# An expert layer whose elementwise work all runs on VectorE, with GpSimd left to gather rows, and the tables of a state space layer made in another place

## The chip, the core and the metric

The kernel runs on one core of a Trainium2 chip. A core has five engines with queues of their own, each worked off in order: TensorE (PE in the rows; PEld is its weight load), VectorE (DVE), ScalarE (ACT), GpSimd (POOL) and SyncE (SP), which here only issues DMAs. Matmuls write PSUM; everything else works in SBUF. The metric is the device time of one execution in microseconds.

## What is computed

Two blocks of a network run over 512 tokens of width 1024, in f32. The first is a mixer followed by a layer of product-key experts; the second is attention, a squared-ReLU MLP, a state space layer (S5) and another such MLP, each followed by a layer norm. What matters here is the expert layer, the first MLP and the tables that the S5 layer reads:

```python
def peer(h, wq, k1, k2, u, v):
    q = (tok @ wq).reshape(-1, 8, 2, 128)                  # 8 heads
    v1, i1 = lax.top_k(q[:, :, 0] @ k1.T, 16); v2, i2 = ...
    cand = v1[..., :, None] + v2[..., None, :]
    top_s, top_c = lax.top_k(cand, 16)
    expert = i1[top_c // 16] * 128 + i2[top_c % 16]        # of 16384 experts
    gate = softmax(top_s)
    act = gelu(sum(x * u[expert]))                         # 128 experts per token
    return sum(gate * act * v[expert])

def sq_relu_mlp(h, w1, b1, w2, b2):
    a = relu(h @ w1 + b1)
    return (a * a) @ w2 + b2

# S5: for 64 groups of 64 states, exp(a dt), cos, sin and products with b and c
# give the tables with which the scan over the tokens is done
```

## The kernel before

Every f32 product is made of three products of a "high" and a "low" part: `split` (L363) takes a weight block of 128x1024 that a DMA brought (`raw`), casts it on ScalarE to `whi` (L366) and subtracts on an elementwise engine to give `wlo` (L367). `eng` chooses that engine: VectorE, unless GpSimd is passed. `proj` and `mm3` then issue 24 matmuls for a block (8 k-chunks, three products each). Activations are split in the same way (`split_act`: cast L493 on ScalarE, subtraction L494 on VectorE, tiles `ahi` and `alo`).

The expert layer `peer` treats 384 of the 512 tokens densely and 128 by gathering.

- **Dense tokens.** The 16384 experts are 128 chunks of 128. For a chunk, `hidden` makes the 24 matmuls `pu` of `u` with the tokens, then a GELU on ScalarE into `hx`. The first `len(AHEAD)` chunks, 80 of them, are made while the experts are being chosen, and written to DRAM (`he`). The rest follow later, in line.
- **Choosing.** `select` makes the scores (`ps_q`) and the top 16 on VectorE (`rank`, `experts`). `spread` then builds a gate for every token and expert chunk with one-hot matrices (L1320, L1321 on VectorE, L1323 and L1329 on ScalarE, `pg` matmuls L1327) and writes them to DRAM (`gd`).
- **Groups.** `grouped` goes over 16 groups of 8 chunks. For each chunk `act` brings `hx` back or makes it, multiplies it by its gates (L1063), and `split_act` makes `ahi` and `alo`, in 9 buffers each. Eight blocks of `v` with 24 matmuls `ps` each follow, and `emit` adds the result to `res` (L1096).
- **Gathered tokens.** `gathered` is a generator that is advanced between the other steps: 128 times an indirect DMA on GpSimd's queue brings one row of `u` per token (L1102) and VectorE reduces it against the token (L1123), then 128 times a row of `v` is fetched and added (L1138). These VectorE instructions are kept in program order. Three `rows` buffers are shared by all.
- **Tables.** `s5_tables` is another generator, advanced between groups 6 to 14. It has about 300 small VectorE instructions, some of ScalarE and TensorE (L1719, L1742), and DMAs of its results to DRAM. `S5In` loads the first two of eight sets of tables at the start of the first MLP.

The first MLP (`mlp`) works in four groups of 8 chunks as well: 24 matmuls `ps_f` a chunk, ReLU on ScalarE, the square on GpSimd (L1416), the split, then 8 blocks with 24 matmuls `ps`. Beside it `mod_columns` computes 48 columns of a modulation by 96 VectorE reductions (L519) over tiles `modw`, which have two buffers and are kept in program order.

The order on each engine is not the order of the code: the framework's scheduler places instructions by a time line of its own, except those kept in order.

## Time and profile before

| what | value |
|---|---|
| median of 3 runs | 3735.75 us (3727.42 to 3742.15) |
| profiled execution | 3738.89 us |
| its span | 3737.1 us |
| busy in the span | PE 3429.7 (92%), DVE 2611.3 (70%), ACT 1601.4 (43%), POOL 1417.7 (38%) us |
| DMA | 635 MB, mean 170 GB/s |

The stages, from the span's start: the mixers end at about 1019 us; choosing experts and spreading gates runs to 1650; the groups to 2507; attention to 2698; the layer norm and the first MLP to 3087; the S5 layer and the second MLP to the end. A matmul counts as busy until its modelled end, so a busy PE is an upper bound of its work.

### The profile page before, as it was taken

How to read it: one execution, taken by the hardware profiler on the slowest of the kernel's cores; microseconds unless marked ns; L12 is line 12 of the kernel's file. 1: busy time of each engine (PE TensorE's matmuls, PEld its weight loads, DVE VectorE, ACT ScalarE, POOL GpSimd, SP SyncE). 2: the span in 40 equal slices, each digit the busy share in tenths (PEclk: the TensorE clock that was granted, in tenths of full speed). 3: DMA queues.
4: the chain of work that ended last, by engine and by line, in shares of the span. 5: the costliest groups of instructions: out<-in, count | busy, mean ns of one | idle time of the engine just before them, and what ended most of it. 6: DMA issues, size and time to landing. Idle time of an engine off the chain costs nothing.

```text
span 3737.1 us, 49602 instructions
## 1 busy us (share of the span) xinstructions
PE 3429.7 (92%) x18337; PEld 3000.6 (80%) x18337; DVE 2611.3 (70%) x4302; ACT 1601.4 (43%) x2482; POOL 1417.7 (38%) x1020
## 2 busy tenths in 40 slices
PE   8999989998998699968899998988989998899998
PEld 5888878877888699958889988986677777777886
DVE  5566675355559999979988989877586536774334
ACT  5565634563332259953333333343442233243333
POOL 3111100111235567745566656544071116353113
PEclk9999999999999899979999998999999999799999
DMA  5223273114325658886888888861156533722332
GB/s 198 80 91 97 88 261 107 51 46 151 100 93 183 203 171 323 309 293 229 287 288 286 286 295 278 276 208 64 34 169 199 185 107 113 203 91 90 96 95 69
DMA packets 264530, 634.97 MB, mean 170 GB/s; under 512 B 33440, under 2 KB 111392, under 8 KB 263904
## 3 DMA queue, kind: packets, MB, share of 16 engines
q1 hardware_dynamic: 216672, 489.18, 39.9%
q0 software_dynamic: 38144, 138.43, 10.5%
q10 hardware_dynamic: 9472, 4.20, 0.4%
q8 instruction: 144, 2.36, 0.3%
q14 instruction: 98, 0.80, 0.1%
HBM read 572.51 MB, written 63.39 MB: 170 GB/s over the span
## 4 chain that ended last, share of the span: by engine, by line
PE 34%; DVE 9%; DMA 6%; issue 5%; POOL 4%; ACT 4%; SPq 0%; POOLq 0%; ACTq 0%; DVEq 0%
PE ps L379 18%; PE ps_f L379 7%; PE ps L412 2%; DMA modw<-in_modT_dram 2%; POOL rows L1102 2%; DVE gacc L1138 1%; ACT o L1323 1%; DVE wlo L367 1%; PE pu L379 1%; DMA raw<-in_u_dram 1%; POOL hx L1063 1%; ACT gs L1329 1%; PE ps_g L379 1%; POOL wlo L367 1%; DVE nx L285 1%
## 5 line engine op out<-in xcount | busy, mean ns | idle before, releaser
L366 ACT CAST whi<-raw 128x1024 fp32r<-128x1024 f32 x547 | 573.1, 1050 | 1031.4 <-PE ps L379 344.8
L367 DVE TENSOR_TENSOR wlo<-raw,whi 128x1024 fp32r<-128x1024 f32 x389 | 501.0, 1291 | 269.5 <-ACT whi L366 154.9
L367 POOL TENSOR_TENSOR wlo<-raw,whi 128x1024 fp32r<-128x1024 f32 x158 | 406.6, 2578 | 231.3 <-ACT whi L366 137.2
L379 PE MATMUL ps<-ahi,whi 128*128 128x384 f32 (+2 forms) x1560 | 349.7, 362 | 98.4 <-ACT ahi L493 80.4
L379 PEld LDWEIGHTS ps<-ahi,whi 128*128 128x128 f32 x1560 | 281.6, 196 | 133.5 <-ACT ahi L493 91.6
L379 PE MATMUL ps<-alo,whi 128*128 128x384 f32 (+2 forms) x1560 | 341.0, 357 | 16.9 <-DVE alo L494 16.8
L379 PE MATMUL ps<-ahi,wlo 128*128 128x384 f32 (+2 forms) x1560 | 325.9, 351 | 0.0
L379 PEld LDWEIGHTS ps<-alo,whi 128*128 128x128 f32 x1560 | 285.5, 196 | 40.1 <-DVE alo L494 19.9
L379 PEld LDWEIGHTS ps<-ahi,wlo 128*128 128x128 f32 x1560 | 276.7, 191 | 20.9 <-issue 0.2
L1416 POOL TENSOR_TENSOR relu<-relu 128x512 f32<-128x512 f32 x64 | 87.5, 1368 | 506.6 <-ACT relu L1415 502.1
L1102 POOL DMA_INDIRECT rows<-in_u_rows_dram,gidx x128 | 181.0, 1414 | 218.2 <-DVE gact L1123 125.4
L1102 POOL DMA_INDIRECT rows<-in_v_rows_dram,gidx x128 | 175.3, 1370 | 199.9 <-DVE gacc L1138 174.4
L1123 DVE CUSTOM_DVE_ANT_0 rows<-rows,gx 128x1024 f32<-128x1024 f32 x128 | 234.9, 1843 | 9.2 <-DMA rows<-in_u_rows_dram,gidx 9.2
L379 PE MATMUL pu<-h_hi,wlo 128*128 128x384 f32 x1024 | 210.6, 347 | 26.1 <-POOL wlo L367 26.1
L379 PE MATMUL pu<-h_hi,whi 128*128 128x384 f32 x1024 | 209.9, 346 | 21.1 <-ACT hx L1041 21.1
L1138 DVE SCALAR_TENSOR_TENSOR gacc<-rows,ggate,gacc 128x1024 f32<-128x1024 f32 x127 | 207.1, 1631 | 25.0 <-DMA rows<-in_v_rows_dram,gidx 24.7
L379 PEld LDWEIGHTS pu<-h_hi,wlo 128*128 128x128 f32 x1024 | 184.4, 194 | 29.9 <-POOL wlo L367 29.9
L379 PEld LDWEIGHTS pu<-h_hi,whi 128*128 128x128 f32 x1024 | 184.2, 194 | 24.3 <-ACT hx L1041 23.3
L379 PE MATMUL pu<-h_lo,whi 128*128 128x384 f32 x1024 | 202.8, 338 | 0.0
L379 PEld LDWEIGHTS pu<-h_lo,whi 128*128 128x128 f32 x1024 | 180.4, 189 | 0.2 <-issue 0.2
L1063 POOL TENSOR_TENSOR hx<-gt,hx 128x384 f32<-128x384 f32 x128 | 158.1, 1247 | 46.5 <-ACT hx L1041 27.1
L1356 DVE SCALAR_TENSOR_TENSOR res<-ps,mod,res 128x512 f32<-128x512 f32 (+1 forms) x92 | 62.2, 677 | 143.0 <-PE ps L379 132.9
(617 smaller groups left out, 7476.1 us busy)
## 6 DMA issues: line engine op xcount, KB each, us to landing
raw<-in_u_dram SPq DMA_DIRECT2D x128, 512.0 KB
raw<-in_v_dram SPq DMA_DIRECT2D x128, 512.0 KB
raw<-in_w_dram SPq DMA_DIRECT2D x128, 512.0 KB
modw<-in_modT_dram SPq DMA_DIRECT2D x192, 256.0 KB
gd<-gs SPq DMA_DIRECT2D x32, 768.0 KB
gt<-gd SPq DMA_DIRECT2D x32, 768.0 KB
raw<-in_w_hg_dram SPq DMA_DIRECT2D x32, 512.0 KB
res<-in_adaT_dram SPq DMA_DIRECT2D x64, 256.0 KB
```

The lines of the kernel that those rows point to most:

```text
L285: nc.vector.scalar_tensor_tensor(out=t[:], in0=res[:, k, tok], scalar=self.g[:, k:k + 1], in1=r[:], op0=ALU.mult, op1=ALU.mult)
L366: self.nc.scalar.copy(out=hi[:], in_=raw[:])
L367: (eng or self.nc.vector).tensor_tensor(out=lo[:], in0=raw[:], in1=hi[:].bitcast(F32), op=ALU.subtract)
L379: self.nc.tensor.matmul(ps, lhsT=w[a], rhs=x[b], start=start and n == 0, stop=stop and n == last)
L412: self.nc.tensor.matmul(ps[:, tok], lhsT=w[a][:, k], rhs=rhs(k, b, tok), start=(k == 0 and i == 0), stop=(k == 7 and i == 2))
L1063: nc.gpsimd.tensor_tensor(out=xb, in0=gt, in1=xb, op=ALU.mult)
L1102: self.nc.gpsimd.indirect_dma_start(out=t[:], out_offset=None, in_=self.ia[rows], in_offset=bass.IndirectOffsetOnAxis(ap=self.gidx[:, s:s ...
L1123: i = nc.vector.tensor_tensor_reduce(out=r[:], in0=r[:], in1=x[:], scale=1.0, scalar=0.0, op0=ALU.mult, op1=ALU.add, accum_out=act[:, s:s ...
L1138: i = nc.vector.scalar_tensor_tensor(out=acc[:], in0=r[:], scalar=w, in1=acc[:], op0=ALU.mult, op1=ALU.add)
L1323: nc.scalar.activation(out=o2[:, j], in_=o2[:, j], func=AF.Copy, scale=gt[:, t0 + j:t0 + j + 1])
L1356: self.nc.vector.scalar_tensor_tensor(out=self.res[:, d, tok], in0=ps, scalar=self.gate1(n)[:, d:d + 1], in1=self.res[:, d, tok], op0=ALU. ...
L1416: nc.gpsimd.tensor_tensor(out=r[:], in0=r[:], in1=r[:], op=ALU.mult)
```

## The change

GpSimd keeps only the gathers in the expert layer: the `wlo` subtraction of 13 query blocks and 128 `u` blocks and the 128 gate products go to VectorE. `rows` has six buffers in place of three. 96 chunks are made ahead in place of 80. The tables are made in the first MLP, from its chunks 1, 4, 7 to 31, and `S5In` loads the first two sets before its last group's tail. A few scratch tiles share a buffer to make room.

```diff
-AHEAD = [8 * g + i for i in range(8) for g in range(16)][:80]
+AHEAD = [8 * g + i for i in range(8) for g in range(16)][:96]
+ROWS = 6
...
         self.B, self.M, self.got = B, M, {}
-        for c in range(2):
-            self.load(c)
...
-            def hidden(e, out, eng=None):
-                w = self.weights(ia["u"][e], eng=eng)
+            def hidden(e, out):
+                w = self.weights(ia["u"][e])
...
-                hidden(e, x[:], nc.gpsimd)
+                hidden(e, x[:])
                 nc.sync.dma_start(out=he[i], in_=x[:])
...
-                        hidden(e, x[:], nc.gpsimd)
+                        hidden(e, x[:])
                     xb = x[:].rearrange("p (b t) -> p b t", b=GBLK)
-                    nc.gpsimd.tensor_tensor(out=xb, in0=gt, in1=xb, op=ALU.mult)
+                    nc.vector.tensor_tensor(out=xb, in0=gt, in1=xb, op=ALU.mult)
...
-                tabs = [tc.tile_pool(name="s5t", bufs=1), tc.tile_pool(name="s5tp", bufs=1, space=PSUM)]
-                tables = self.s5_tables(*[p.__enter__() for p in tabs], self.s5dram)
...
-                    if 6 <= g < 15:
-                        next(tables, None)
...
-        t = self.A.tile([128, D], F32, tag="rows", bufs=3, name="rows")
+        t = self.A.tile([128, D], F32, tag="rows", bufs=ROWS, name="rows")
...
-                    w = self.weights(ia["w_q"][hd * 2 + p], eng=nc.gpsimd)
+                    w = self.weights(ia["w_q"][hd * 2 + p])
...
-        m = M.tile([128, n], F32, tag=f"rest{n}", bufs=3, name="rest")
+        m = M.tile([128, n], F32, tag=f"rest{n}", bufs=2, name="rest")
...
-            if n == 1:
-
-                ins = self.tc.tile_pool(name="s5in", bufs=1)
-                self.tables = S5In(self, ins.__enter__())
...
             row = self.mod_row(mt, ia["crow2"])
             modT = ia["modT"].rearrange("a b p k -> (a b) p k")
+            tabs = [self.tc.tile_pool(name="s5t", bufs=1), self.tc.tile_pool(name="s5tp", bufs=1, space=PSUM)]
+            tables = self.s5_tables(*[p.__enter__() for p in tabs], self.s5dram)
...
                 self.mod_columns(mt, row, modT, range(48 + 2 * f, min(96, 50 + 2 * f)), self.col("modb", 0, 96), self.mod2)
+                if f % 3 == 1:
+                    next(tables, None)
...
             if g == 3 and i == 0:
-                mods.__exit__(None, None, None)
+                for p in tabs[::-1] + [mods]:
+                    p.__exit__(None, None, None)
+                self.ins = self.tc.tile_pool(name="s5in", bufs=1, side="right")
+                self.tables = S5In(self, self.ins.__enter__())
+                for c in range(2):
+                    self.tables.load(c)
```

**GpSimd in the groups.** Ahead of the change, this is its queue over about one group: gathers (`rows`), gate products (`hx`) and the low parts of `u` blocks (`wlo`) in turn.

```order
L1063 TENSOR_TENSOR hx<-gt,hx 128x384 x4
L1102 DMA rows<-in_v_rows_dram,gidx 128x1024
L1063 TENSOR_TENSOR hx<-gt,hx 128x384
L1102 DMA rows<-in_v_rows_dram,gidx 128x1024 x3
L367 TENSOR_TENSOR wlo<-raw,whi 128x1024
L1102 DMA rows<-in_v_rows_dram,gidx 128x1024 x2
L367 TENSOR_TENSOR wlo<-raw,whi 128x1024 x2
```

With the change this is its queue for the whole expert layer, with the last instruction ahead of it (of the first three query blocks) and the first behind it (of the attention's first blocks). Line numbers are now those of the changed kernel.

```order
L366 TENSOR_TENSOR wlo<-raw,whi 128x1024 x3
L1093 DMA rows<-in_u_rows_dram,gidx 128x1024 x128
L1093 DMA rows<-in_v_rows_dram,gidx 128x1024 x128
L366 TENSOR_TENSOR wlo<-raw,whi 128x1024 x3
```

Nothing but gathers stands between the two.

**VectorE where one group ends and the next begins.** Before: the low halves `alo` of the next group's activations, with gathered sums (`gacc`), one `wlo` of a `v` block and pieces of the tables (`s_...`) between them.

```order
L1138 SCALAR_TENSOR_TENSOR gacc<-rows,ggate,gacc 128x1024
L494 TENSOR_TENSOR alo<-hx,ahi 128x384 x3
L1738 COPY s_bbz<-s_bb_17038 64x4x16 x2
L1744 COPY s_kz<-spk 32x4x128
L1463 SCALAR_TENSOR_TENSOR s_rot<-s_an 128x256
L1738 COPY s_bbz<-s_bb_17039 64x4x16
L494 TENSOR_TENSOR alo<-hx,ahi 128x384
L1738 COPY s_bbz<-s_bb_17039 64x4x16
L1138 SCALAR_TENSOR_TENSOR gacc<-rows,ggate,gacc 128x1024
```

With the change, at the same place:

```order
L493 TENSOR_TENSOR alo<-hx,ahi 128x384 x2
L366 TENSOR_TENSOR wlo<-raw,whi 128x1024
L1129 SCALAR_TENSOR_TENSOR gacc<-rows,ggate,gacc 128x1024
L366 TENSOR_TENSOR wlo<-raw,whi 128x1024
L1062 TENSOR_TENSOR hx<-gt,hx 128x384
L1129 SCALAR_TENSOR_TENSOR gacc<-rows,ggate,gacc 128x1024
L366 TENSOR_TENSOR wlo<-raw,whi 128x1024
L1062 TENSOR_TENSOR hx<-gt,hx 128x384
L493 TENSOR_TENSOR alo<-hx,ahi 128x384
```

The tables are gone, and the gate products and the `wlo` of the `u` blocks stand between the `alo` of one group. On TensorE the matmuls `pu` that lie at each such border are 72 before and 48 now.

**VectorE in the first MLP**, in the eight `w2` blocks of the first group. Before: the result (`res`), the low half of the next block, and the modulation's reductions (`modw`).

```order
L519 ISA modw,mod_89<-modw,sc_row_23698,cols 128x512
L519 ISA mod_89 128x1
L1356 SCALAR_TENSOR_TENSOR res<-ps,mod_89,res 128x512
L367 TENSOR_TENSOR wlo<-raw,whi 128x1024
L519 ISA modw,mod_89<-modw,sc_row_23699,mod_89 128x512
```

With the change:

```order
L1343 SCALAR_TENSOR_TENSOR res<-ps,mod_89,res 128x512
L366 TENSOR_TENSOR wlo<-raw,whi 128x1024
L1729 SCALAR_TENSOR_TENSOR s_cp<-s_cp,s_t_23362 128x576
L1700 TENSOR_TENSOR s_an<-s_tr,s_iota 128x256
L518 ISA modw,mod_89<-modw,sc_row_23028,mod_89 128x512
L518 ISA mod_89 128x1
L1343 SCALAR_TENSOR_TENSOR res<-ps,mod_89,res 128x512
L366 TENSOR_TENSOR wlo<-raw,whi 128x1024
L518 ISA modw,mod_89<-modw,sc_row_23027,cols 128x512
```

The tables' instructions stand between the reductions and ahead of the next `wlo`. The first part of the tables, about a hundred instructions of 32 to 512 elements, stands earlier still, among those of the layer norm ahead of this MLP.

## Rows read from the trace of the kernel before

**Rows 1.** Stages: start:end, length, busy us (instructions) of PE, PEld, DVE, ACT, POOL; PEclk, DMA share, GB/s

```profile
1019.00:1631.00 612.00, 544.47 (x3193) 519.24 (x3193) 543.68 (x1182) 360.29 (x701) 370.48 (x179) 0.95 0.64 218
1111.00:1320.00 209.00, 159.46 (x836) 154.12 (x835) 208.30 (x757) 58.50 (x77) 117.49 (x62) 0.90 0.60 189
1374.00:1631.00 257.00, 241.75 (x1607) 236.90 (x1605) 241.32 (x202) 246.90 (x545) 179.24 (x89) 0.98 0.84 302
1650.00:2507.00 857.00, 768.75 (x4234) 745.54 (x4233) 765.36 (x896) 303.51 (x411) 503.04 (x343) 0.95 0.80 272
2698.00:3087.00 389.00, 370.06 (x1691) 301.66 (x1690) 241.35 (x385) 128.78 (x168) 104.69 (x92) 0.98 0.52 165
```

**Rows 2.** PE in 1650:2507: busy us, mean ns | idle before, and who ended it

```profile
L379 PE MATMUL ps<-ahi,whi 128*128 128x384 f32 x962 | 215.9, 359 | 98.4 <-ACT ahi L493 80.4 <-issue 8.0 <-DVE res L1096 5.0
L379 PE MATMUL ps<-alo,whi 128*128 128x384 f32 x960 | 202.8, 350 | 8.2 <-DVE alo L494 8.2
...
L1742 PE MATMUL spk<-s_cp,s_bbz 128*32 128x128 f32 x128 | 17.0, 276 | 0.0
L1719 PE MATMUL spt<-ident,s_s 128*128 128x128 f32 x64 | 12.6, 317 | 0.0
```

**Rows 3.** Waits in 1640:2507: who waited for whom, total us, times, longest us

```profile
ACT ahi L493 <- POOL hx L1063: 206.5, 60, 17.3
```

**Rows 4.** Timeline from 1990 us: start, length in us, engine, line, operation

```profile
1995.15 0.48 ACT L1041 ACTIVATE hx<-pu 128x384 f32<-128x384 f32 x1
1995.42 1.28 DVE L1138 SCALAR_TENSOR_TENSOR gacc<-rows,ggate,gacc 128x1024 f32<-128x1024 f32 x1
1996.19 1.32 POOL L1102 DMA_INDIRECT rows<-in_v_rows_dram,gidx  x1 [0.30 <-issue]
...
2003.41 0.55 DVE L494 TENSOR_TENSOR alo<-hx,ahi 128x384 fp32r<-128x384 f32 x1
...
2004.60 3.75 DVE L1714 TENSOR_TENSOR s_s<-s_s,s_t 128x512 f32<-128x512 f32 x1
2004.84 2.96 POOL L1063 TENSOR_TENSOR hx<-gt,hx 128x384 f32<-128x384 f32 x3
...
2009.94 1.21 DVE L367 TENSOR_TENSOR wlo<-raw,whi 128x1024 fp32r<-128x1024 f32 x1
```

**Rows 5.** DVE in 1650:2507, by line: busy us, mean ns | idle before

```profile
L1138 DVE SCALAR_TENSOR_TENSOR gacc<-rows,ggate,gacc 128x1024 f32<-128x1024 f32 x127 | 207.1, 1631 | 25.0 <-DMA rows<-in_v_rows_dram,gidx 24.7
L367 DVE TENSOR_TENSOR wlo<-raw,whi 128x1024 fp32r<-128x1024 f32 x122 | 163.2, 1339 | 7.3 <-ACT whi L366 6.4 <-PE pu L379 0.9
L494 DVE TENSOR_TENSOR alo<-hx,ahi 128x384 fp32r<-128x384 f32 x128 | 106.2, 849 | 36.8 <-ACT ahi L493 35.2 <-issue 1.4
L1123 DVE CUSTOM_DVE_ANT_0 rows<-rows,gx 128x1024 f32<-128x1024 f32 x47 | 78.7, 1678 | 4.5 <-DMA rows<-in_u_rows_dram,gidx 4.5
L1096 DVE SCALAR_TENSOR_TENSOR res<-ps,mod,res 128x384 f32<-128x384 f32 x122 | 74.1, 608 | 30.5 <-PE ps L379 29.5 <-PE ps L412 0.5
```

**Rows 6.** DVE in 1080:1640, by line

```profile
L1123 DVE CUSTOM_DVE_ANT_0 rows<-rows,gx 128x1024 f32<-128x1024 f32 x81 | 156.2, 1939 | 4.8 <-DMA rows<-in_u_rows_dram,gidx 4.8
L1320 DVE TENSOR_TENSOR o<-tr,iota 128x1024 f32<-128x1024 f32 x48 | 70.5, 1471 | 11.4 <-PE pg L1327 8.0 <-issue 2.2 <-ACT gs L1329 0.9
L1321 DVE TENSOR_TENSOR o<-tr,iota 128x1024 f32<-128x1024 f32 x48 | 67.0, 1395 | 0.5 <-PE pt L1298 0.5
```

**Rows 7.** Chain that ended last: start us, length us, engine, tile and line, matmuls

```profile
2166.04 21.08 PE ps L379 x120
...
2485.90 12.70 PE pu L379 x72
```

**Rows 8.** Waits in 2690:3160, which holds the first MLP

```profile
DVE modw L519 <- DMA modw<-in_modT_dram: 61.1, 46, 3.2
```

**Rows 9.** GpSimd in 2690:3160, its costliest line

```profile
L1416 POOL TENSOR_TENSOR relu<-relu 128x512 f32<-128x512 f32 x32 | 42.4, 1326 | 261.1 <-ACT relu L1415 256.6 <-DVE alo L494 4.6
```

**Rows 10.** DMA queue SP in 1650:2507: what its issues waited for

```profile
SPq L1745 <- DVE s_kz L1744: 32.5, 7, 10.7
```

More of the change, by code (lines that the diff above doesn't have):

```diff
@@ L1081, in between @@
                             pass
-                    if 6 <= g < 15:
-                        next(tables, None)
-                    if g == 15:
-                        for p in tabs[::-1]:
-                            p.__exit__(None, None, None)
                 def emit(d, ps, tok):
@@ L1110, in gathered @@
         x = A.tile([128, D], F32, tag="gx", bufs=1, name="gx")
-        f = A.tile([128, D], F32, tag="rows", bufs=3, name="gf")
+        f = A.tile([128, D], F32, tag="rows", bufs=ROWS, name="gf")
         nc.vector.tensor_tensor(out=f[:].rearrange("p (k t) -> p k t", k=8), in0=self.h[0][:, :, GATHERED].bitcast(F32),
@@ L1237, in experts @@
             v = nc.vector
-            new = lambda name, dt=F32: S.tile([128, n], dt, tag=f"{name}{n}", bufs=1, name=name)
+            new = lambda name, dt=F32: S.tile([128, n], dt, tag=f"{name}", bufs=1, name=name)
             flat = lambda t: t[:, c0:c1].rearrange("p c h r -> p (c h r)")
@@ L1255, in experts @@
                 key = new(f"key{p}")
-                num = S.tile([128, n], F32, tag=f"num{n}", bufs=1, name="num")
+                num = S.tile([128, n], F32, tag="num", bufs=1, name="num")
                 v.tensor_copy(out=num[:], in_=flat(idx[p]))
@@ L1267, in experts @@
                 out.append(key)
-            gate, den = new("gate"), S.tile([128, n // 16], F32, tag=f"den{n}", bufs=1, name="den")
+            gate, den = new("gate"), S.tile([128, n // 16], F32, tag="den", bufs=1, name="den")
             h16 = lambda a: a[:].rearrange("p (h r) -> p h r", r=16)
@@ L1346, in block2 @@
         for n in range(4):
-            if n == 1:
-                ins = self.tc.tile_pool(name="s5in", bufs=1)
-                self.tables = S5In(self, ins.__enter__())
             if n == 3:
-                ins.__exit__(None, None, None)
+                self.ins.__exit__(None, None, None)
             with self.tc.tile_pool(name=f"lay{n}", bufs=1) as M, \
```

## The prediction

> **What bounds the kernel now.** I read the stages first, since an average over the whole span mixes different limits [rows 1]. Two of the changed stages are bound by TensorE: the groups (768.75 of 857 us busy) and the first MLP (370.06 of 389). Choosing and spreading is mixed: over all of it PE and DVE are busy alike (544.47 and 543.68 of 612 us), but from 1111 to 1320 VectorE is full (208.30 of 209), and from 1374 to 1631 ScalarE is (246.90 of 257). The granted clock is 0.95 to 0.98 over the TensorE-bound stages, so their matmuls run near the upper level, and I change nothing for it.
>
> Next I read what the idle TensorE of the groups waits for. 857 - 769 leaves 88 us, and the waits for `ahi` (80.4) and `alo` (8.2) make up all of it [rows 2]. `ahi` is ScalarE's cast, and ScalarE in turn waited 206.5 us, up to 17.3 us at a time, for GpSimd's gate product `hx` [rows 3]. So the stage has a queue behind it that the change empties: the product on GpSimd behind gathers and `wlo`.
>
> Last I read single durations, because the same VectorE instruction has two prices [rows 4]. `gacc` beside a gather on GpSimd takes 1.28 us; `s_s`, half as large, takes 3.75 us beside three products on GpSimd. Alone, `alo` takes 0.55 and `wlo` 1.21. The means in the groups are above these: `gacc` 1.631, `alo` 0.849, `wlo` 1.339 [rows 5]; while the experts are chosen, the gathered reduction takes 1.939 and the one-hot build 1.471, both of 128x1024 elements [rows 6]. VectorE pays for a GpSimd that computes, and hardly for one that gathers.
>
> **Prices.** A matmul of 384 columns costs 21.08/120 = 0.176 us on the chain, and 12.70/72 = 0.176 where the inline chunks stand [rows 7]. On VectorE I take the prices without GpSimd: 1.28 for `gacc`, 1.21 for `wlo` and for the other operations of 128x1024, 0.55 for `alo`. The gate product on VectorE is not in the trace. It has the shape and the two SBUF inputs of `alo`, hence 0.55; the mean of `alo` as it is now, 0.849, bounds it above.
>
> **Choosing and spreading.** 16 more chunks are made here, 384 matmuls: 67.6 us. PE then has 544.5 + 67.6 = 612 us of work in a stage of 612, so all of it must fit the present holes. VectorE gains 111 `wlo` (13 query blocks and the 98 chunks that now stand ahead of the first group's matmuls): 134 us. It loses the surcharge: 81 x (1.939 - 1.21) = 59 us on the reductions and 48 x (1.471 - 1.21) = 12 on L1320, with some more on its twin L1321 and on smaller operations, which I don't count. 544 + 134 - 71 = 607 of 612. Both engines are near full, and neither is over: the low bound is 0. The high bound is what the two full stretches would add if nothing of it found a hole: while VectorE is full, 836 matmuls, or 35 chunks, are made [rows 1], and their `wlo` are 35 x 1.21 = 42 us; while ScalarE is full, 16 more GELUs of 0.48 are 8 us. That makes +50. I take **+18**, about a third of it: the surcharge goes in the first of these stretches too, and ScalarE loses 20 of its 160 loads of activation tables in the change, 12 of them at the GELU's line, which help to pay for the second.
>
> **The groups.** PE loses 24 matmuls at each of 15 borders and those of one chunk of the first group: 384 x 0.176 = 67.6 us, and the tables' transposes and products, 17.0 + 12.6 = 29.6 us [rows 2]. 768.75 - 97.2 = 671.5 us of matmuls are left. Of the idle 88 us I keep 50. At each of 15 borders, the last inline chunk goes through GELU (0.48), product (0.55), cast (about 0.5, as a tile of the same size in the GELU) and `alo` (0.55), 2.1 us, and in VectorE's queue a `gacc` or a `wlo`, some 1.2 us, stands ahead of one of these: 3.3 x 15 = 50. The cover for the chunks before it shrinks too: from 72 matmuls (12.7 us) to 48 (8.4), in which VectorE has seven `alo`, up to two products, and the `gacc` and `wlo` between them, some 10 us at the prices alone. Most of the `alo` of chunks that come from DRAM can stand earlier, in the group before, as one buffer more than a group needs exists.
>
> Whether VectorE keeps up decides the rest. Its bill in the groups: `gacc` 127 x 1.28 = 163, the 47 reductions x 1.21 = 57, `wlo` (122 + 30) x 1.21 = 184, `alo` 128 x 0.55 = 70, products 128 x 0.55 = 70, `res` 122 x 0.608 = 74. Together 618 us, below 671.5. The tables are no longer in it: they are the difference between 765.36 and the five lines' 629.3, **136 us** [rows 1, 5]; I use 130, as some pairs of small results of other lines are in it. So PE bounds the groups: 671.5 + 50 = 721, a gain of 857 - 721 = **-136 us**. Bounds: with the present 88 us of idle, 760 and -97; with VectorE at today's means (127 x 1.631 + 47 x 1.678 + 152 x 1.339 + 128 x 0.849 twice + 74 = 781) at least 781 and some 9 of idle, so -67; with 19 us of idle in place of 50, -167. Loads: 272 GB/s over 857 us is 233 MB; less 16 blocks of `u` of 0.5 MB it is 225, in 721 us 312 GB/s. The spread stretch moves 302 at a share of 0.84 [rows 1], so the queues carry it, without much reserve.
>
> **The first MLP.** PE gets the tables' 29.6 us. VectorE gets their 130 us: 241 + 130 = 371 of 389, not counting that its reductions stand still for `modw` for 61.1 us [rows 8], since they have two buffers and a fixed order; 371 + 61 = 432. The tables' DMAs now stand in SyncE's queue beside those of `modw` and the weights. In the groups that queue stood 32.5 us in seven waits for `s_kz` [rows 10]; here a load behind such a wait comes late by up to 10.7 us, and the cover is the raw buffers ahead. What waits behind the tables on VectorE are the next block's `wlo`, and so PE. I take 29.6 plus as much idle again as the stage has, 389 - 370 = 19: **+49**; the sum of VectorE, 432 - 389 = 43, lies beside it. Low bound: PE's 29.6 fill the 19 first, +11. High bound: 432 and the whole of the 42.4 us in which GpSimd squares [rows 9], as a lock on VectorE, +85.
>
> On this term a rule of the Trainium skill speaks against the change. Rows 4 show a table instruction with two SBUF inputs at 3.75 us beside GpSimd's products, and `gacc` unchanged beside a gather. The skill's page "SBUF — State Buffer", section "Who interferes with whom", says that a VectorE instruction with two SBUF inputs contends with a GpSimd instruction that reads SBUF, that the second to issue blocks fully, and that one that only writes does no harm. By it the squares in the MLP, whose input and output are in SBUF, would lock the tables as the products did in the groups, and the term would be +85, the time 3706; by the rows alone it is +49. The trace of before has no table instruction beside a square, so it neither agrees nor speaks against it. I give this case 0.15 of the forecast's 0.55 below.
>
> **The sum.** 18 - 136 + 49 = -69. Against the profiled execution of 3738.9 this is **3670 us**; the median of the runs lies 3 us lower, 3667, which I count as the same.
>
> **The rivals.**
>
> First, VectorE inherits the wait. Products stand in a strict queue behind `gacc`, and `gacc` itself waits for gathers (24.7 us of VectorE's idle time now [rows 5]); ScalarE then waits for VectorE as it did for GpSimd, the 88 us stay, and in the MLP the tables hold up `wlo` at the high bound. For it: the order at the borders puts two `gacc` and three `wlo` among the last products. Against it: six `rows` buffers instead of three, and GpSimd free of all else. 18 - 97 + 85 = +6: 3745 us, the same. Chance 0.17.
>
> Second, slower: the two prices of VectorE have another cause than GpSimd's arithmetic, say the traffic of the gathers or of the weights, and stay. It decides when `gacc` stays near 1.6 us with only gathers on GpSimd. Then choosing has 544 + 134 = 678 us of VectorE in 612, +66; the groups are bound by VectorE, 790, -67; the MLP is at +85. Together +84: 3823 us. For it: the means are averages, and traffic grows. Against it: the 1.28 us beside a gather [rows 4]. Chance 0.13.
>
> Third, more than forecast: the waits at the borders shrink to 19 us and choosing costs nothing, since the surcharge was larger than what I counted, and the MLP costs only PE's matmuls, 30. -167 + 30 = -137: 3602 us. For it: at 618 of 671 VectorE has slack, and the product's queue is two instructions deep. Against it: 8.4 us of cover instead of 12.7. Chance 0.15.
>
> **How the numbers follow.** The forecast has 0.55, with its terms anywhere between their bounds. About 0.5%, 19 us, is what a measurement of this kernel can tell from no change. Faster: the forecast nearly whole, the third rival, and a little of the first, 0.73; the same, most of the first and the edge of the forecast, 0.13; slower, the second and the edge of the first, 0.14. The range reaches from the third rival, 3600, to just over the first, 3755; outside lie the second and the half of the third that goes further.
>
> **What would show it.** In the changed profile: on GpSimd only gathers between the third query block and the attention; `gacc` near 1.28, `alo` near 0.55, `wlo` near 1.21, the reductions near 1.21 (at today's means the second rival is right). The groups last about 721 us and PE waits for `ahi` and `alo` for some 50 (near 88 is the first rival, below 20 the third). Choosing to the first group lasts about 18 us longer. From the attention's end to the S5 layer it takes about 438 us, PE waiting for `wlo`, VectorE still for `modw`. The forecast falls if the MLP grows by over 85 us, if the squares lock the tables, or if the groups become bound by loads at some 300 GB/s.

## The result

The changed kernel takes 3599.89 us in the median (3597.06 to 3603.72), against 3737.02 (3727.42 to 3742.15) for the kernel before: a ratio of 0.964, interval 0.9615 to 0.9658, 137 us or 3.7% less. The forecast was 3670; the low end of the range, 3600, was missed by a tenth of a microsecond. The sign was as forecast, and TensorE still bounds the groups and the MLP as forecast; the gain is twice as large, and nearly all of the miss lies in the groups. The profiled execution takes 3601.07 us, its span 3599.3.

The stages of the changed kernel, in the columns of [rows 1], cut at the events that cut them there:

```profile
1017.00:1631.00 614.00, 593.78 (x3577) 572.71 (x3577) 516.03 (x1290) 386.16 (x733) 121.03 (x85) 0.99 0.69 239
1110.00:1313.00 203.00, 201.05 (x1158) 200.01 (x1157) 199.45 (x804) 79.15 (x104) 37.48 (x30) 1.00 0.74 247
1375.00:1631.00 256.00, 237.88 (x1587) 232.21 (x1585) 206.42 (x231) 245.12 (x538) 77.92 (x52) 0.98 0.81 300
1646.00:1700.00 54.00, 40.77 (x199) 38.68 (x200) 41.45 (x71) 12.24 (x17) 21.54 (x17) 0.80 0.82 278
1646.00:2310.00 664.00, 643.35 (x3656) 637.49 (x3657) 572.52 (x763) 230.13 (x312) 251.58 (x171) 0.98 0.89 317
1700.00:2290.00 590.00, 582.58 (x3341) 578.84 (x3340) 517.65 (x668) 209.43 (x281) 230.05 (x154) 1.00 0.91 327
2501.00:2589.00 88.00, 62.81 (x372) 55.29 (x370) 84.39 (x173) 32.85 (x53) 60.18 (x60) 0.90 0.26 85
2589.00:2945.00 356.00, 340.09 (x1504) 268.75 (x1505) 275.75 (x504) 116.17 (x161) 48.14 (x35) 0.98 0.66 205
```

Choosing and spreading lasts 614 us in place of 612, though 16 more chunks are made in it, and the groups 664 in place of 857. The attention lasts 191 in both. From there the two kernels are cut once more, since the layer norm and the MLP went different ways; the same stretches before:

```profile
2698.00:2765.00 67.00, 57.13 (x370) 51.24 (x368) 58.62 (x78) 28.47 (x47) 52.80 (x52) 0.95 0.54 158
2765.00:3087.00 322.00, 312.93 (x1321) 250.41 (x1322) 182.73 (x307) 100.31 (x122) 51.89 (x41) 0.98 0.51 167
```

The layer norm takes 88 us in place of 67, the MLP 356 in place of 322, the stretch to the S5 layer 69 in place of 67 (2945 to 3014 and 3087 to 3154). From the first matmul of the S5 layer on it is 585 and 583. The sum is -2 (choosing, with the gap ahead of the first group) - 193 (groups) + 57 (layer norm, MLP and the stretch to S5) + 2 = -136, the difference of the spans to within 2 us.

VectorE in the groups (1646:2310), columns as in [rows 5]:

```profile
L366 DVE TENSOR_TENSOR wlo<-raw,whi 128x1024 fp32r<-128x1024 f32 x151 | 183.3, 1217 | 17.4 <-ACT whi L365 17.1
L1129 DVE SCALAR_TENSOR_TENSOR gacc<-rows,ggate,gacc 128x1024 f32<-128x1024 f32 x127 | 162.1, 1276 | 0.0
...
L1062 DVE TENSOR_TENSOR hx<-gt,hx 128x384 f32<-128x384 f32 x127 | 69.2, 552 | 42.3 <-DMA hx<-he 42.0
L493 DVE TENSOR_TENSOR alo<-hx,ahi 128x384 fp32r<-128x384 f32 x128 | 66.1, 550 | 7.2 <-ACT ahi L492 7.2
L1114 DVE CUSTOM_DVE_ANT_0 rows<-rows,gx 128x1024 f32<-128x1024 f32 x49 | 59.5, 1215 | 4.0 <-DMA rows<-in_u_rows_dram,gidx 4.0
```

Every price is the one taken in the prediction: 1.276, 0.550, 1.217, 1.215, and 0.552 for the product on VectorE, which [rows 4] could give only by its likeness to `alo`. On GpSimd nothing but the two times 128 gathers is left. TensorE in the same stretch:

```profile
L378 PE MATMUL ps<-ahi,whi 128*128 128x384 f32 x960 | 193.3, 341 | 36.2 <-ACT ahi L492 32.0 <-DVE res L1087 4.2
```

32.0 us of waiting for `ahi` are left of 80.4 [rows 2], and they are nearly all the first group's (16.2 of them end at 1646, ahead of the stage, as 18.9 of the 80.4 end ahead of 1650 in the kernel before). Waits of TensorE from 1700 to 2290, in which nearly all the borders lie:

```profile
PE ps L378 <- DVE res L1087: 4.2, 5, 1.5
PE ps L378 <- ACT ahi L492: 2.5, 4, 1.2
PE ps L378 <- DVE alo L493: 0.7, 1, 0.7
```

2.5 us for `ahi`. At six of the borders the chain that ended last goes from `pu` to `ps` on TensorE alone, as here (start, length, what):

```profile
1826.50 8.33 PE pu L378 x48
1834.84 33.31 PE ps L378 x192
```

8.33 us of inline chunks, 33.31 of `v` blocks, no gap between: 0.1735 us for a matmul, at a granted clock of 1.00. At the others it leaves TensorE at a short wait and follows VectorE and the loads of `hx`; all waits from 1700 to 2290 together are the 7.4 us above. The border at 1834, in the timeline (start, length):

```profile
1834.67 4.00 PE L378 MATMUL ps<-ahi,whi 128*128 128x384 f32 x22
...
1837.46 0.52 ACT L492 CAST ahi<-hx 128x384 fp32r<-128x384 f32 x1 [1.70 <-DVE hx L1062]
...
1838.52 1.37 PE L378 MATMUL ps<-alo,whi 128*128 128x384 f32 x7
1839.02 0.55 DVE L493 TENSOR_TENSOR alo<-hx,ahi 128x384 fp32r<-128x384 f32 x1
```

The cast of the last chunk's `ahi` begins at 1837.46, 2.6 us after the last `pu` ends, and its `alo` at 1839.02. TensorE meanwhile issues 22 products of `ahi` with `whi` over three blocks of `v` (the kernel has three buffers for their results): seven each for the first two, without the last chunk, and all eight for the third. The two that are missing follow singly, behind products with `alo`.

### The profile page after: what moved, and what is told of

It is laid out like the page before. It is cut to its first block, busy times and chain, and to the rows that moved or that the text cites. A ratio compares the mean times of both kernels' runs of the same rounds, so it can differ in the third digit from the quotient of the medians.

```text
span 3599.3 us, 49485 instructions
## 1 busy us (share of the span) xinstructions
PE 3389.1 (94%) x18337; PEld 2971.2 (83%) x18337; DVE 2510.4 (70%) x4571; ACT 1575.0 (44%) x2462; POOL 915.5 (25%) x751
## 4 chain that ended last, share of the span: by engine, by line
PE 35%; DVE 8%; DMA 6%; issue 2%; ACT 1%; POOL 1%; SPq 1%; DVEq 0%; ACTq 0%; POOLq 0%
PE ps L378 18%; PE ps_f L378 6%; PE pu L378 3%; PE ps L411 2%; DMA hx<-he 2%; DMA modw<-in_modT_dram 1%; DVE wlo L366 1%; PE ps_g L378 1%; DVE modw L518 1%; DVE nx L286 1%; DMA d_rot<-s_rot 1%; PE ps_s L1570 1%; PE ps_s L1569 1%; PE ps_qb L378 1%; DVE h_lo L496 1%
## 5 line engine op out<-in xcount | busy, mean ns | idle before, releaser
L366 DVE TENSOR_TENSOR wlo<-raw,whi 128x1024 fp32r<-128x1024 f32 x530 | 656.8, 1242 | 328.5 <-ACT whi L365 208.0
L378 PE MATMUL ps<-ahi,whi 128*128 128x384 f32 (+2 forms) x1560 | 330.5, 352 | 42.3 <-ACT ahi L492 36.1
L378 PE MATMUL ps<-alo,whi 128*128 128x384 f32 (+2 forms) x1560 | 332.6, 350 | 0.7 <-DVE alo L493 0.7
L378 PEld LDWEIGHTS ps<-alo,whi 128*128 128x128 f32 x1560 | 275.7, 190 | 21.8 <-DVE alo L493 1.0
L1093 POOL DMA_INDIRECT rows<-in_v_rows_dram,gidx x128 | 196.1, 1532 | 275.5 <-DVE gacc L1129 254.0
L378 PE MATMUL pu<-h_hi,wlo 128*128 128x384 f32 x1024 | 201.6, 337 | 0.0
L1129 DVE SCALAR_TENSOR_TENSOR gacc<-rows,ggate,gacc 128x1024 f32<-128x1024 f32 x127 | 162.1, 1276 | 0.0
L1114 DVE CUSTOM_DVE_ANT_0 rows<-rows,gx 128x1024 f32<-128x1024 f32 x128 | 154.2, 1217 | 5.9 <-DMA rows<-in_u_rows_dram,gidx 5.9
L378 PE MATMUL ps_f<-h_hi,whi 128*128 128x512 f32 x464 | 120.7, 402 | 1.2 <-ACT whi L365 1.2
L378 PE MATMUL ps_f<-h_hi,wlo 128*128 128x512 f32 x464 | 120.3, 399 | 0.0
```

The costliest lines, as they stand in the source:

```text
L366: (eng or self.nc.vector).tensor_tensor(out=lo[:], in0=raw[:], in1=hi[:].bitcast(F32), op=ALU.subtract)
L378: self.nc.tensor.matmul(ps, lhsT=w[a], rhs=x[b], start=start and n == 0, stop=stop and n == last)
L1093: self.nc.gpsimd.indirect_dma_start(out=t[:], out_offset=None, in_=self.ia[rows], in_offset=bass.IndirectOffsetOnAxis(ap=self.gidx[:, s:s ...
L1114: i = nc.vector.tensor_tensor_reduce(out=r[:], in0=r[:], in1=x[:], scale=1.0, scalar=0.0, op0=ALU.mult, op1=ALU.add, accum_out=act[:, s:s ...
L1129: i = nc.vector.scalar_tensor_tensor(out=acc[:], in0=r[:], scalar=w, in1=acc[:], op0=ALU.mult, op1=ALU.add)
```

## The experiments

Eleven kernels ran. Each is timed beside the kernel before, whose median lay between 3734.5 and 3737.3 us there; the changed kernel was not timed again, so a difference of a few us from it says nothing. Times are medians. For stages I give the time from the first score matmul to the first `v` matmul as choosing, from there to the last `v` matmul of 384 columns as groups (three blocks beyond the stage above), from the attention's last matmul to the first one of the S5 layer as MLP (with the layer norms ahead of it and behind it). The stages are those of each kernel's one profiled execution:

| kernel | time, us | ratio, interval | choosing | groups | MLP |
|---|---|---|---|---|---|
| before | 3737.0 | | 630 | 870 | 455 |
| changed | 3599.9 | 0.9615 to 0.9658 | 629 | 677 | 512 |
| 80 chunks (e1) | 3628.7 | 0.9685 to 0.9728 | 603 | 730 | 512 |
| products on GpSimd (e2) | 3611.8 | 0.9644 to 0.9687 | 631 | 684 | 514 |
| low parts on GpSimd (e3) | 3650.6 | 0.9736 to 0.9792 | 662 | 696 | 510 |
| both on GpSimd (e4) | 3678.4 | 0.9817 to 0.9864 | 662 | 724 | 508 |
| three row buffers (e5) | 3612.4 | 0.9647 to 0.9685 | 628 | 692 | 509 |
| e5, tables in the groups (e6) | 3641.1 | 0.9723 to 0.9764 | 629 | 767 | 471 |
| before, tables moved (e7) | 3717.2 | 0.9925 to 0.9967 | 634 | 787 | 515 |
| tables tied (e8) | 3580.6 | 0.9568 to 0.9607 | 628 | 675 | 494 |
| e8, squares on ScalarE (e9) | 3572.3 | 0.9550 to 0.9582 | 627 | 676 | 485 |
| e8, 104 chunks (e10) | 3604.1 | 0.9636 to 0.9668 | 641 | 683 | 495 |
| before, VectorE only (e11) | 3619.6 | 0.9669 to 0.9701 | 605 | 781 | 453 |

**The chunks made ahead (e1).**

```diff
-AHEAD = [...][:96]
+AHEAD = [...][:80]
```

> The changed kernel with 80 chunks ahead in place of 96, all else as changed. 384 matmuls of 0.174 us, 66.7 us, go back to the groups. Theory 1 (what the 16 chunks put into choosing fell into holes of TensorE there, so choosing gives nothing back): groups 664 + 67 to 75, choosing 629 as it is, 3600 + 70 = 3670 us. Theory 2 (TensorE is full from 1110 to 1313, 201 of 203 us, so choosing is now bound by TensorE in that stretch and shrinks without them): choosing 600, groups 735, 3640 us. The prediction's own terms (-68 in the groups, +18 in choosing) say 3650.

The spread stage of this kernel and its groups:

```profile
1379.00:1607.00 228.00, 192.05 (x1201) 183.37 (x1199) 188.50 (x215) 220.20 (x505) 76.79 (x52) 0.90 0.78 286
...
1623.00:2340.00 717.00, 708.03 (x4037) 703.28 (x4038) 593.10 (x778) 254.45 (x344) 248.17 (x171) 0.99 0.86 301
```

3628.7: the groups are 53 us longer, but choosing is 26 shorter. Theory 2's sign was right, its place wrong. It is not the stretch in which TensorE is full that shrinks (359 us from the first score to the first gate matmul in both) but the spread, from 254 to 228: ScalarE is full there (220.20 of 228), and each chunk adds a cast and a GELU to it. The 16 chunks are worth 29 us, where the terms of the prediction said 50 (-68 and +18).

**What GpSimd's arithmetic costs (e2, e3, e4).** e2 has the first of these edits, e3 the second and third, e4 all three:

```diff
-nc.vector.tensor_tensor(out=xb, in0=gt, in1=xb, op=ALU.mult)
+nc.gpsimd.tensor_tensor(out=xb, in0=gt, in1=xb, op=ALU.mult)
...
-w = self.weights(ia["u"][e])
+w = self.weights(ia["u"][e], eng=nc.gpsimd)
...
-w = self.weights(ia["w_q"][hd * 2 + p])
+w = self.weights(ia["w_q"][hd * 2 + p], eng=nc.gpsimd)
```

> The changed kernel with the gate products alone back on GpSimd. Theory 1 (GpSimd's arithmetic makes VectorE slow and its products come late behind gathers): the means of gacc, alo and wlo in the groups rise above 1.28, 0.55 and 1.21 again, TensorE waits for ahi for 60 us or more in place of 32, groups +50, 3650 us. Theory 2 (with wlo gone, GpSimd's queue is short enough and VectorE is 69 us lighter): within 10 us of 3600. Theory 3 (the two prices of VectorE have another cause, as in the second rival): the means stay at 1.28, 0.55 and 1.21 also with products on GpSimd.

> The changed kernel with the low parts of the 13 query and 128 u blocks alone back on GpSimd. Theory 1 (they cost choosing its speed, by the wait of TensorE for them, 25 us in 1111 to 1320 of before, and by slowing the gathered reductions beside them to 1.9 us): choosing 629 + 45, groups +10, 3655 us. Theory 2 (VectorE was no bound there and gains the time that it loses): choosing within 10 us, 3605 us.

> The changed kernel with both, products and low parts, back on GpSimd: what is left of the change is the six row buffers, the 96 chunks and the tables in the first MLP. Theory 1 (the engine is what the change is about): the sum of the two before it, +100, 3700 us. Theory 2 (the tables and the chunks carry the gain): 3620 us.

VectorE in the groups, first with the products on GpSimd (e2), then with both (e4):

```profile
L366 DVE TENSOR_TENSOR wlo<-raw,whi 128x1024 fp32r<-128x1024 f32 x151 | 211.8, 1405 | 12.6 <-ACT whi L365 12.4
L1129 DVE SCALAR_TENSOR_TENSOR gacc<-rows,ggate,gacc 128x1024 f32<-128x1024 f32 x127 | 194.6, 1532 | 0.2
L493 DVE TENSOR_TENSOR alo<-hx,ahi 128x384 fp32r<-128x384 f32 x128 | 87.7, 714 | 34.5 <-ACT ahi L492 34.5
```

```profile
L1129 DVE SCALAR_TENSOR_TENSOR gacc<-rows,ggate,gacc 128x1024 f32<-128x1024 f32 x127 | 215.2, 1694 | 0.4
L366 DVE TENSOR_TENSOR wlo<-raw,whi 128x1024 fp32r<-128x1024 f32 x122 | 165.4, 1359 | 9.4 <-ACT whi L365 9.3
L493 DVE TENSOR_TENSOR alo<-hx,ahi 128x384 fp32r<-128x384 f32 x128 | 113.5, 914 | 21.7 <-ACT ahi L492 21.7
```

The products alone lift `wlo` from 1.217 to 1.405, `gacc` from 1.276 to 1.532, `alo` from 0.550 to 0.714, with the same gathers beside them; with both on GpSimd `gacc` is at 1.694 and `alo` at 0.914, above what they were before. The second price of VectorE thus comes from GpSimd's arithmetic, and the second rival is out.

In time the products alone cost only 12 us (theory 2 was nearer than theory 1's 50): with 69 us of products gone from VectorE the locked prices still fit. The low parts cost 51, two thirds of it in choosing (629 to 662), nearer to theory 1 of that run than to theory 2; but the stretch from the first score to the first gate matmul is no longer (356 us against 358). TensorE gets through 1587 matmuls in it in place of 1992, waiting 33.7 us for `wlo` from GpSimd, and the chunks left over lengthen the spread by 9 us and the time from the last gate matmul to the first `v` matmul from 16 to 43. Both cost 79, less than theory 1's 100 but more than the sum of the two apart.

**The row buffers (e5)**, `ROWS = 3`:

> The changed kernel with three buffers for the gathered rows in place of six. Theory 1 (with the products in VectorE's queue, a late gather stops them, as the first rival had it, and six buffers prevent that): gacc's idle time in the groups rises from 0.0 to 20 us or more, groups +15, 3615 us. Theory 2 (VectorE has 664 - 572 = 92 us of slack there and the gathers come in time): within 5 us of 3600.

`gacc` then stands idle for 28 us for a gather (0.0 with six), and the groups last 15 us longer:

```profile
L1129 DVE SCALAR_TENSOR_TENSOR gacc<-rows,ggate,gacc 128x1024 f32<-128x1024 f32 x127 | 162.6, 1280 | 28.1 <-DMA rows<-in_v_rows_dram,gidx 27.9
```

Theory 1, in its number too. What the first rival described, a late gather that stops the products behind it, exists, but is small, and the six buffers take it away.

**The tables (e6, e7).** In e6 their pools and steps stand in the expert layer again as in the kernel before; e7 is the changed kernel with 80 chunks, three row buffers and GpSimd's two operations, so that the tables, with the scratch tiles that make room for them and the place where the first two sets are loaded, are all that differs from before.

> The changed kernel with three row buffers (there is no room for six beside them) and the tables made in groups 6 to 14 again, to be held against the run with three row buffers alone. VectorE's bill in the groups is then 572 + 130 = 702 us, TensorE's 634 + 30. Theory 1 (taking the tables out of the groups is where the larger part of the gain is: VectorE would be their bound): groups 664 to 740, the first MLP 57 shorter, 3620 us. Theory 2 (the tables cost the groups TensorE's 30 us and little else, as the prediction had it): groups 700, the MLP 57 shorter, 3580 us, less than the changed kernel.

> The kernel before with one part of the change alone, the tables made in the first MLP (80 chunks, three row buffers, products and low parts on GpSimd). Theory 1 (in the groups of before VectorE, slowed by GpSimd, was full where the tables stood, so they cost the groups 90 us): groups 870 - 90 with their last blocks, MLP + 57, 3705 us. Theory 2 (the tables cost TensorE's 30 us and little else): groups -30 to -40, MLP +57, 3755 us, slower than before.

The groups of e6, and TensorE in the groups of e7:

```profile
1647.00:2402.00 755.00, 689.66 (x3850) 672.34 (x3851) 684.21 (x1058) 273.79 (x376) 253.32 (x174) 0.95 0.89 305
```

```profile
L378 PE MATMUL ps<-ahi,whi 128*128 128x384 f32 x968 | 201.1, 343 | 64.7 <-ACT ahi L492 63.7 <-ACT whi L365 0.7
```

Theory 1 in both, and in e6 more than it. In e6 the tables lengthen the groups by 75 us against e5, in e7 their removal shortens them by 83. TensorE's matmuls for them are 30 of that. The rest is waiting and a lower granted clock (0.95 in e6, 0.98 in the changed kernel): of the 65 us in which TensorE is idle in e6, 33 are waits for `ahi` and 22.4 are one wait at the end for the last gathered sum, with VectorE 684.21 of 755 us busy. (The profiled execution of e6, whose stages these are, is 10 us above its median.) In e7 the waits for `ahi` stay at 63.7, with the products still on GpSimd (39.3 in e11, with products and low parts on VectorE and the tables left where they were). The MLP pays 59 for the tables there, so that moving them gives only 17 us by itself (3734.5 to 3717.2). In e6 the MLP gives back 38 and not 57; 11 of the difference stand in the layer norm ahead of it (78 us against 67 before), though no table instruction is there any more. Why stays open.

**The tables tied to the MLP (e8).** The hundred small instructions that begin the tables stand among the layer norm's in the changed kernel. VectorE there (start, length; the idle time before it, if any, at the end):

```profile
2523.68 1.70 DVE L1604 TENSOR_TENSOR ep<-ep,er 128x32 f32<-128x32 f32 x1
...
2528.04 2.27 DVE L252 TENSOR_TENSOR nsq<-nsq,nt 128x512 f32<-128x512 f32 x1
2530.23 1.28 DVE L1604 TENSOR_TENSOR ep<-ep,er 128x32 f32<-128x32 f32 x1
```

`ep` is the tables', `nsq` the layer norm's, and `nsq`, 0.68 us elsewhere, takes 2.27 beside this `wlo` on GpSimd:

```profile
2527.38 2.39 POOL L366 TENSOR_TENSOR wlo<-raw,whi 128x1024 fp32r<-128x1024 f32 x1 [0.73 <-ACT whi L365]
```

TensorE's waits in 2501 to 2589 (the same two were 2.0 and 2.8 us in the kernel before):

```profile
PE nps L266 <- DVE nsq L252: 11.4, 2, 8.9
PE ps L411 <- DVE h_lo L496: 7.7, 8, 2.8
```

In e8 the tables' input is first copied, and the copy is kept in order behind the modulation's reductions of chunk 4; the steps come from chunk 4 on in place of chunk 1, which was not tried apart:

```diff
-lr, li = st[:, 1], st[:, 2]
+raw, st = st, M.tile([128, 3, 32], F32, name="s_st")
+self.tc.keep_in_program_order(v.tensor_copy(out=st[:], in_=raw[:]))
+lr, li = st[:, 1], st[:, 2]
...
-if f % 3 == 1:
+if f in (4, 7, 10, 13, 16, 19, 22, 25, 28):
```

> The changed kernel in which the tables begin with a copy of their input that is kept in order behind the modulation's reductions of the first MLP's chunk 4, so that their first hundred small instructions can't stand among those of the layer norm ahead of it; the loops come from chunks 7 to 28. Theory 1 (these instructions delay the layer norm, which grew from 67 us, attention's end to the first matmul of the MLP, to 88): this stretch falls to 67 to 70, the MLP doesn't grow by as much, 3582 us. Theory 2 (the work is only moved, and the MLP behind it takes it up in full): 3600 us.

```profile
2501.00:2569.00 68.00, 57.37 (x363) 51.19 (x364) 59.64 (x78) 28.87 (x48) 53.78 (x54) 0.95 0.34 110
2569.00:2925.00 356.00, 341.68 (x1532) 269.58 (x1531) 298.91 (x602) 119.93 (x166) 52.95 (x43) 0.99 0.62 194
```

Theory 1: the layer norm is back at 68 us, and the MLP takes the hundred instructions in without growing (356 as in the changed kernel, VectorE 299 of it in place of 276). 3580.6 us beats both kernels.

**The squares (e9).** On top of e8, in the first MLP:

```diff
-nc.gpsimd.tensor_tensor(out=r[:], in0=r[:], in1=r[:], op=ALU.mult)
+nc.scalar.activation(out=r[:], in_=r[:], func=AF.Square)
```

> The kernel with the tied tables (e8) in which the first MLP's squares stand on ScalarE in place of GpSimd. Theory 1 (GpSimd's squares lock VectorE's instructions with two inputs, as its products did in the groups): the mean of wlo in the first MLP falls from 1.28 to 1.21, VectorE's bill there falls by 10 to 40 us and the MLP by up to 15, 3570 us. Theory 2 (TensorE bounds the MLP, 342 of 356 us, and VectorE, 299 of 356, has room for the lock): within 5 us of 3580.

VectorE in the MLP, in e8 and in e9, and the MLP of e9:

```profile
L366 DVE TENSOR_TENSOR wlo<-raw,whi 128x1024 fp32r<-128x1024 f32 x58 | 75.0, 1294 | 6.0 <-ACT whi L365 3.7 <-PE ps_f L378 2.1
```

```profile
L366 DVE TENSOR_TENSOR wlo<-raw,whi 128x1024 fp32r<-128x1024 f32 x58 | 71.8, 1239 | 7.6 <-PE ps_f L378 3.9 <-ACT whi L365 3.2 <-issue 0.5
```

```profile
2565.00:2915.00 350.00, 341.28 (x1536) 269.96 (x1536) 282.06 (x602) 138.63 (x198) 14.60 (x11) 1.00 0.65 201
```

The lock is there: `wlo` falls from 1.294 to about 1.24, the reductions (`modw`) from 0.819 to 0.757, VectorE's bill from 298.91 to 282.06. The MLP is 6 us shorter of it, and of the 8 us between the medians the rest lies outside (the stages differ by 1 to 4 us each between the two runs); the intervals, 0.9568 to 0.9607 and 0.9550 to 0.9582, overlap. So theory 1 holds for the lock and, by its "up to 15", for the stage, though `wlo` does not come down to 1.21; the whole time does not tell the two kernels apart clearly.

**More chunks (e10)**, e8 with `[:104]`:

> The kernel with the tied tables (e8) with 104 chunks ahead. From 80 to 96 the spread stage grew by 27 us and the groups fell by 53. Theory 1 (the same rate goes on): spread + 13, groups - 27, 3567 us. Theory 2 (the groups, with 317 GB/s at a share of 0.89 and TensorE waiting for hx from DRAM, are bound by loads from here on, and every chunk brought back adds one): spread + 13 to 35, groups - 10 or nothing, 3585 to 3600 us.

```profile
1661.00:2332.00 671.00, 627.61 (x3490) 621.47 (x3491) 565.35 (x757) 220.19 (x298) 255.65 (x171) 0.96 0.87 311
1700.00:2000.00 300.00, 271.52 (x1487) 269.00 (x1486) 247.29 (x349) 93.24 (x126) 118.53 (x81) 0.95 0.90 318
2000.00:2320.00 320.00, 317.22 (x1819) 316.26 (x1819) 283.99 (x350) 113.59 (x152) 124.14 (x81) 0.99 0.89 318
```

TensorE's waits in the groups, and in 1700 to 2000:

```profile
PE ps L378 <- ACT ahi L492: 58.6, 14, 18.7
```

```profile
PE ps L378 <- ACT ahi L492: 27.9, 7, 5.8
```

24 us slower. The groups have 29 us less of matmuls (168 of 0.174) and last 8 us longer: TensorE waits 58.6 us for `ahi`, 18.7 of them ahead of the stage. That is theory 2's time, beyond its range by 4, but not its reason. Seven borders, all before 2000 us, now have one inline chunk, 24 matmuls `pu`, and TensorE waits at every one of them, 27.9 us in all, at a granted clock of 0.95; the borders behind 2000 still have two, and there it is busy for 317 of 320 us. The loads run at 318 GB/s in both stretches, and in e8 at 334 from 1700 to 2000 without such waits. A load of `hx` takes 6.1 us from issue to landing in the median in both kernels there. So the queues' rate is not the bound. The place is the border with one inline chunk: it has half the cover and a seventh chunk to bring back, and at five of the seven the product that the next cast waits for starts 0.6 to 2.3 us late for its load. Cover and loads come together in this edit and were not taken apart.

**The elementwise part alone (e11).** The kernel before with the two edits of e4 turned round:

> The kernel before with the elementwise part of the change alone: products and low parts on VectorE; 80 chunks, three row buffers, and the tables in the groups stay. Theory 1 (the parts add up: choosing - 33 and the groups - 48, as the two on GpSimd cost in the changed kernel): 3655 us. Theory 2 (with the tables there VectorE, at some 620 + 130 us, inherits the wait at the borders, as the first rival had it): groups no more than 20 us shorter, choosing - 30, 3690 us.

```profile
1623.00:2391.00 768.00, 741.47 (x4232) 726.41 (x4233) 698.43 (x1071) 299.69 (x407) 274.53 (x174) 0.99 0.88 305
```

```profile
L379 PE MATMUL ps<-ahi,whi 128*128 128x384 f32 x960 | 200.5, 344 | 42.1 <-ACT ahi L493 39.3 <-DVE res L1096 2.3 <-ACT whi L366 0.3
```

3619.6, better than both theories. This part alone takes 117 us off: 25 in choosing and 89 in the groups, where VectorE, 698.43 of 768 with the tables, doesn't become the bound. The first rival is out.

Where the 25 us of choosing come from, before and in e11 (first score to first gate matmul, then e11's spread):

```profile
1019.00:1374.00 355.00, 302.72 (x1588) 282.34 (x1589) 302.36 (x980) 113.39 (x157) 191.23 (x91) 0.93 0.50 157
```

```profile
1018.00:1376.00 358.00, 356.22 (x1995) 340.81 (x1994) 309.31 (x1059) 141.28 (x198) 41.26 (x30) 1.00 0.58 192
1376.00:1605.00 229.00, 192.98 (x1200) 183.60 (x1198) 188.51 (x215) 218.84 (x504) 79.15 (x52) 0.90 0.77 280
```

The first stretch is as long as before, but TensorE, which waited 25.5 us for `wlo` from GpSimd in it, now makes 407 matmuls more there. So the spread has 17 chunks fewer to make. ScalarE, which fills it (246.90 of 257 us before [rows 1]), is spared their casts and GELUs, 17 x (1.06 + 0.51) = 27 us, and the spread is 28 us shorter.

## Why the prediction was right and wrong

Along one path through the runs the change is: products and low parts on VectorE, -117 (e11); tables moved and six row buffers, +9 (e1 against e11: groups -51, MLP +59); 16 more chunks, -29 (changed against e1). The parts are not additive: undone last, the tables' move takes 29 us off (e5 against e6), and beside tables in the groups 16 more chunks cost choosing 24 us and save the groups 14 (e6 against e11).

**The prices and what bounds the groups** held. VectorE's bill of 618 us is 614 by the six lines of the changed kernel (the five shown and `res` with 73.9; 572.52 busy, where overlapping instructions count once), below TensorE's 643, which is the bound. Loads at 317 GB/s and a share of 0.89 did not stop it. The rule of the Trainium skill that the prediction draws on ("SBUF — State Buffer", "Who interferes with whom"), that a VectorE instruction with two SBUF inputs contends with a GpSimd instruction that reads SBUF, agrees with e2, e4 and e9: with products on GpSimd `gacc` rises from 1.276 to 1.532, with gathers alone it doesn't.

**The groups, -136 forecast, -193 measured: this term failed, at two steps.** The first is the idle time. I kept 3.3 us at each of 15 borders, 50 in all, as though the chain through GELU, product, cast and `alo` of the last chunk stood in the open. The trace shows 2.5 us of waiting for `ahi` and 0.7 for `alo` at all the borders after 1700: the products of the chunks that are there, three blocks ahead, cover the chain of the last. e10 shows where that ends: with 24 matmuls `pu` at a border in place of 48, and one more chunk to load, TensorE waits again. The reading of before was off too: the waits for `ahi` and `alo` do not make up all of the 88 us, since 18.9 of the 80.4 end ahead of the stage; inside it 61.5 stand for `ahi`, 8.2 for `alo` and some 18 for others. Of the 20.7 us of idle that are left (664 - 643.35), 13 stand in the first 54 us.

The second is TensorE's work. I subtracted 384 matmuls at 0.176 and the tables' from 768.75 and kept the other 3658 at 671.5/3658 = 0.184 each, as if they would cost the same without the stalls. The granted clock was 0.95 there, and I wrote that I change nothing for it. Without stalls it is 1.00 from 1700 on, a matmul takes 0.174 there (582.58/3341), and 643.35 are left in the stage, not 671.5. 29 us of idle time (50 - 20.7) and 28 of price (671.5 - 643.35) are the whole miss of 57.

With these steps goes the share of each part. The elementwise part was to bring 38 us in the groups (88 - 50); it brings 89 (e11): TensorE's idle time falls from 88 to 27 us (768 - 741.47), and its busy time on the same matmuls from 768.75 to 741.47, with the granted clock at 0.99 in place of 0.95. The tables were priced at TensorE's 30 us in the groups; their move gives 51 (e1 against e11, with the row buffers) to 83 (e7).

**Choosing, +18 forecast, -2 measured.** Two errors that nearly cancel. For the 16 chunks I expected holes and ScalarE's table loads to pay; they cost 26 us in the spread (e1). VectorE's surcharge I took as 71 us, by two lines; its bill fell from 543.68 to 516.03 with 134 us of `wlo` added, so the refund is about 160 us. The lines that I didn't count, the small ones of the top 16 and of the one-hot sums, were locked too: the three `cand` lines of the top 16 took 66 us and take 16.5. The refund does not shorten VectorE's stretch, it pays for the `wlo` in it; the 25 us that choosing gains come from the chunks that TensorE gets done there ahead of the spread (e11).

**The first MLP with the layer norm, +49 forecast, +55 measured** (+57 with the stretch to S5). The size is right, the place is only half right. I had put the idle time into the MLP; 21 us of it are the layer norm's, delayed by the tables' first hundred instructions, and e8 gives them back. By that rule of the Trainium skill, with the squares' whole time as a lock, the term was 85. The lock is there (e9), but takes 17 us of VectorE and 6 of the stage. A row of before could have sized it: `wlo` in the first MLP, from 2765 to 3087, took 1.283 us in the mean beside the squares, 6% above 1.21.

**The rivals.** The third, more than forecast, is what happened, with about its 19 us of idle time (20.7, but 13 of them in the first group and not at the borders) and nothing for choosing (-2). Its 3602 lies 2 us off the result, though by errors that cancel: 26 us more gained in the groups than it had, 27 more lost in layer norm and MLP. It had a chance of 0.15, and the range ended on it; it should have gone on below.

## To carry over

When stalls go, what stays doesn't keep its price: take the matmuls that remain at the price of an unstalled run of them, and look for the granted clock of a stretch that has none. A chain at a border costs only what the first consumers don't cover, so ask which of them can start without its last piece, and how far ahead the order lets them run; 48 matmuls of inline chunks at a border were enough here, 24 with one more chunk to load were not (e10). A stretch in which an engine is full need not get shorter when that engine gets faster: here another engine got more done beside it, and the next stretch shrank. And work that is moved to a stage with room does harm at the place where the scheduler puts its first instructions: here the layer norm ahead of the stage, and keeping them behind it was worth 19 us.

## What the runs showed of the hardware

GpSimd's tensor operations lift VectorE's instructions with two SBUF inputs by 12 to 66% in the mean in the groups of e2 and e4 (`wlo` 1.217 to 1.359, `alo` 0.550 to 0.914, both in e4), while gathers by DMA on the same queue leave them where they are (0.550, the changed kernel). `res`, which takes one of its two large inputs from PSUM, is not lifted: 0.608 us before, 0.611 in e4, 0.612 in the changed kernel. Short instructions can pay more: the candidate sums of 128x8 took 0.849 us in the mean while experts were chosen before, and take 0.150 in the changed kernel. One with a single input paid too: a TENSOR_SCALAR of 128x32 of the tables (L1608) took 2.38 us in the changed kernel, from 2518.07 to the end of a `wlo` on GpSimd, where the next like it (L1609) took 0.17. A gather's issue itself takes GpSimd 1.4 to 1.5 us in the mean, by the profile's rough spans of that engine:

```profile
L1093 POOL DMA_INDIRECT rows<-in_v_rows_dram,gidx x128 | 196.1, 1532 | 275.5 <-DVE gacc L1129 254.0 <-DVE gact L1114 18.7 <-DVE hx L1062 2.1
L1093 POOL DMA_INDIRECT rows<-in_u_rows_dram,gidx x128 | 176.5, 1379 | 638.7 <-DVE gact L1114 437.7 <-DVE v L1327 182.2 <-issue 7.6
```

And TensorE's granted clock in the groups goes with its idle time: 0.95 with 88 us idle in 857, 0.98 with 21 in 664, 1.00 in the 590 us in which 7 are idle; in e10 it is 0.95 with 28 us idle in 300 and 0.99 with 3 in 320.
